# A decoder layer on one core: turnings by row count, parameter rows in one tile, sinks by a mask, two squares summed by accumulating transfers, state row copies apart

## The chip, the cores and the metric

The kernel runs on one core of a Trainium2 chip. A core has TensorE (PE: matrix products and turnings, that is transposes), VectorE (DVE), ScalarE (ACT), GpSimd (POOL) and SyncE (SP), each with its own in-order instruction stream, and DMA queues that move data between HBM and SBUF. The metric is the device time of one launch in microseconds, as the median of several runs; less is better.

## The reference

One inference step of a hybrid decoder layer, in float32, for 512 prompt tokens and 32 sample tokens (8 sequences of 4 tokens); D_MODEL is 1024, D_FF 4096:

```python
def _layer(x, ...):
    h = _rmsnorm(x, norm_mix_pre)
    x_r, q, k, v, g = split(h @ w_in)                    # one combined projection
    A = RG_LRU(causal_conv(x_r, width 4))                # 8 gate blocks
    B = window_attention(q, k, v)                        # window 128, 8 heads / 2 kv heads
    m = (sigmoid(g_A) * (A @ w_lru_o) + sigmoid(g_B) * (B @ w_attn_o)) @ w_out
    x = x + _rmsnorm(m, norm_mix_post)
    u = causal_conv(_rmsnorm(x, norm_ffn_pre) @ w_up, width 3)
    f = (gelu(u_gate) * u_val) @ w_down
    return x + _rmsnorm(f, norm_ffn_post)
```

In the attention each head has a sink, a number that joins the maximum and the denominator of the softmax, and a bias that depends on the distance in 32 buckets (`rel_bias`). The state rows (LRU state, convolution rows, the key and value window) are outputs too.

## The kernel before

**Numbers.** Each float32 operand of a product is split into a high and a low half (ScalarE makes the high one, VectorE the low one: `wh_*`/`wl_*` for weights, `hH`/`hL` for activations), and a product is three passes: high x high, high x low, low x high. Activations lie transposed: features on the 128 partitions, tokens along the free axis.

**Stages.** Up to 12 us: loads and the first turnings. Then the in-projection (`pmin`) with attention and LRU between its steps up to some 330 us; the two output products of the branches (`pmao`, `pmlo`); `w_out` (`pmout`, about 379 to 430 us); the norms behind it; and the feed-forward part, 430 to 965 us, where the up-projection runs in sums of weight blocks and of token halves (`pq` at first, later `pux`, `puy`, `puz`), the down-projection is `pmdn`, and the end turns the rows back and writes them.

**Order.** TensorE's stream is written out by hand for the whole program. In the first stages the other engines' streams are too: `step` (L344) emits one column block of a projection and then calls `tick` (L194), which runs the generators whose time has come (`start_at`, `sides`) and the lists `mids`, `late` and `last`. In the stage of `w_out` and the norms the tile scheduler orders ScalarE, VectorE and POOL, and `yield` in a generator sets how much TensorE work lies between its parts. Loads of weights go through SP's queue, each of them behind one of eight rotating semaphores; POOL issues its own transfers in its own stream, so that a transfer that waits holds up all that POOL does later.

**Places that the change touches.**
- `turn_b` (L521) turns tokens 256 to 543 to features: for each of four 128-column blocks k, two 128-row tiles and one 32-row tile (the sample tokens) into one PSUM bank `ps_tb`, two such groups of four k in all. The evictions (`hsplit`, `keep_b`) are put on `last` behind them. `xsquares` and `roots` (L533) work out the norm's factor; it is spread over the partitions by a product with a diagonal, `ps_rep <- dg, ones`.
- `relx` and `ohp` (L390 to L393) hold `rel_bias` and a one-hot matrix, 32 rows; their product in `roots` (bank `ps_rep`) picks the bias for each distance.
- `rows_a` and `rows_b` (L371, L573) hold norm and LRU parameters as rows; `params` (L596) turns them, the convolution weights `rows_f` and the state rows `st_rows` to columns.
- `sinkb` holds the sinks on all partitions, `sink8` as 8 rows; `sample_tables` (L659) makes `sinkr`, one sink for each row of the sample's score matrix, by a product with the mask `hsel`.
- `norm_chain` (L1234) works out the two norms behind `w_out` for one token half (a = 0 or 1, columns 0 to 271 and 272 to 543). For a = 1 it adds the scaled rows to the residual x (even c on POOL, odd c on VectorE), squares each of the eight x tiles on ScalarE (`sq_x`; the square of tile 0 goes straight to the sum `acc2`, called accx in the trace) and adds the squares on VectorE; `stats` sums over the partitions with a product (`pst_f`), `diag` and `spread` (`rep_f`) follow, and `normed` makes the operands of the next products. At the same time the splits of the first up-projection weights run on ScalarE and VectorE (`do_high`, `do_low`: `wh_e`, `wl_e`), for the products `pq` on TensorE.
- `ffn_states` (L1736) turns the last up-projected rows back near the end, copies them on ScalarE (`ffn_rows_s`, `ffn_rows_p`), and POOL writes them out.

The transfers that add what they carry to their target occur elsewhere too, in the sums of weight blocks (L1452 and L1453):

```python
pool.dma_start(out=w["p2"], in_=w["p1"], accum_op=ALU.add)
pool.dma_start(out=w["p4"], in_=w["p2"], accum_op=ALU.add)
```

Of the kernel before, what the change touches and what calls it, by code (L numbers as in the profile page):

```python
# [11 lines left out]
F32 = mybir.dt.float32  # L12
# [5 lines left out]
P = 128  # L18
# [11 lines left out]
NH = 8  # L30
# [60 lines left out]
def _shape_constants():  # L91
    t = np.arange(WIN)
    ohp = np.zeros((NBK, WIN), np.float32)
    ohp[_bucket(WIN - 1 - t), t] = 1.0
    ohs = np.zeros((DT, NBK, SKEY), np.float32)
    msk = np.full((2, DB // 2, NH, DT, SKEY), NEG, np.float32)
    for tq in range(DT):
        for kv in range(NKV):
            hs = slice(4 * kv, 4 * kv + 4)
            for j in range(WIN):  # L100
                dd = tq + WIN - j
                if 0 <= dd < WIN:
# [12 lines left out]
    return {  # L115
        "c_ohp": ohp,
        "c_ohs": ohs.reshape(DT * NBK, SKEY),
        "c_msk": msk.reshape(2, P, SKEY),
        "c_hsel": hsel.reshape(NH, P),
    }  # L120


# [1 line left out]
def hawk_step(ctx, tc, I, O):  # L124
# [21 lines left out]
    def T(name, dt=F32):  # L146
        return tp.tile([P, FLAT + 4], dt, tag="t", name=name)
# [7 lines left out]
    def PX(name):  # L155
        return psx.tile([P, 512], F32, tag="aux", name=name)
# [7 lines left out]
    def mm(out, l, r, start, stop):  # L164
        pe.matmul(out, l, r, start=start, stop=stop)  # L165
# [205 lines left out]
    rows_a = cp.tile([32, P], F32, name="rows_a")  # L371
    act.dma_start(out=rows_a[0:8, :], in_=I["norm_mix_pre"].rearrange("o (k p) -> (o k) p", p=P))
    warm = keep.tile([P, 1], F32, name="warm")
    act.activation(warm, epst, AF.Sqrt)
# [12 lines left out]
        nc.sync.dma_start(out=raw0[:, 4 * z:4 * z + 4, :], in_=wsrc(order[0])[:, 4 * z:4 * z + 4, :])  # L387
    wload(1)
    wload(2)
    relx = cp.tile([NBK, NH], F32, name="relx")  # L390
    nc.sync.dma_start(out=relx, in_=I["rel_bias"])
    ohp = T("ohp")[:NBK, 0:WIN]
    nc.sync.dma_start(out=ohp, in_=I["c_ohp"])  # L393
    wload(3)
    for i in (2, 3, 4):
        xload(i)
# [49 lines left out]
    def xtile(i, k):  # L446
        n = TOK[i][1]
        return xt[i, k // 4][:n, (k % 4) * P:(k % 4 + 1) * P]
# [70 lines left out]
    rq = cp.tile([P, 4], F32, name="rq")  # L519

    def turn_b(ks):  # L521
        for k in ks:
            ps = PX(f"ps_tb{k}")
            for i in (2, 3, 4):
                t0, n, _ = TOK[i]
                pe.transpose(ps[:, t0 - 256:t0 - 256 + n], xtile(i, k), ident[:n, :n])  # L526
            tb.append(ps)
            last.append(lambda k=k, ps=ps: hsplit(k, 1, ps[:, :288]))
        last.extend(lambda k=k, ps=tb[k]: keep_b(k, ps) for k in ks)

    ps_ohp = []
# [38 lines left out]
        yield from roots(2, 5)  # L570
        dve.tensor_scalar(rq, ss[:, 1, 0:4], SCALE, None, ALU.mult)

    rows_b = cp.tile([64, P], F32, name="rows_b")  # L573
    nc.sync.dma_start(out=rows_b[0:32, :], in_=I["conv_lru_w"].rearrange("o t (k p) -> (o t k) p", p=P))
    for r, nme in ((32, "conv_lru_b"), (40, "lru_br"), (48, "lru_bi"), (56, "lru_lambda")):
        nc.sync.dma_start(out=rows_b[r:r + 8, :], in_=I[nme].rearrange("o (k p) -> (o k) p", p=P))
# [18 lines left out]

    def params():  # L596
        ps = PX("ps_rows")
        pe.transpose(ps[:, 0:32], rows_a[:, :], ident[:32, :32])
        pe.transpose(ps[:, 32:96], rows_b[:, :], ident[:64, :64])
        pe.transpose(ps[:, 128:256], rows_f[:, 0, :], ident)  # L600
        pe.transpose(ps[:, 256:384], rows_f[:, 1, :], ident)
        px = PX("ps_st")
        for k in range(KD):
            pe.transpose(px[:, k * 32:(k + 1) * 32], st_rows[k // 4][:32, (k % 4) * P:(k % 4 + 1) * P], ident[:32, :32])
        yield
        dve.tensor_copy(pv[:, 8:96], ps[:, 8:96])
        dve.tensor_copy(fv, ps[:, 128:384])
# [27 lines left out]
    sink8 = cp.tile([NH, 1], F32, name="sink8")  # L635
    nc.sync.dma_start(out=sink8, in_=I["attn_sink"].rearrange("o h -> h o"))
    hsel = cp.tile([NH, P], F32, name="hsel")
# [21 lines left out]
    def sample_tables():  # L659
# [10 lines left out]
        yield 2  # L670
        ps = PX("ps_bs")
        mm(ps[:, 0:SKEY], lt.rearrange("p b h t -> p (b h t)"), ohs, True, True)
        mm(ps[:, 384:385], hsel, sink8, True, True)
        yield
        dve.tensor_copy(sinkr, ps[:, 384:385])
        for g in range(2):
            add(biasS[:, g, :], ps[:, 0:SKEY], mk[g])
        yield
# [555 lines left out]
    def norm_chain(a, acc):  # L1234
# [8 lines left out]
        with tc.high_priority(offset=HP):  # L1243
# [12 lines left out]
            for g in range(6 if a else 0):  # L1256
# [7 lines left out]
                for c in range(2 * g - 3, 2 * g - 1) if 1 <= g < 6 else ():  # L1264
                    if 0 <= c < 8:
                        sq[c] = acc2 if c == 0 else T(f"sq_x{a}_{c}")
                        act.activation(sq[c][:, :n], x1_(c), AF.Square)
                        if c == 0 and n % P:
                            pool.memset(acc2[:, n:n + P - n % P], 0.0)
                for c in range(2 * g - 5, 2 * g - 3) if g < 5 else range(5, 8):  # L1270
                    if c > 0:
                        add(acc2[:, :n], acc2[:, :n], sq[c][:, :n])
                yield 0.5
        yield NORM_TICKS[a]
# [461 lines left out]
    def ffn_states():  # L1736
        os_ = O["s_ffn_conv"].rearrange("o b i (m n) -> (o b i m) n", n=D)
        op = O["p_ffn_conv"].rearrange("o b i (m n) -> (o b i m) n", n=D)
        for kk in range(2):
# [4 lines left out]
                pe.transpose(py[:16, j * P:(j + 1) * P], stage_p[:, 4 * kk + j].rearrange("p r m -> p (r m)"), ident)  # L1744
            o1, o2 = S(f"ffn_rows_s{kk}"), S(f"ffn_rows_p{kk}")
            act.copy(o1[:, 0:512], px)
            act.copy(o2[:16, 0:512], py[:16, :])
            pool.dma_start(out=os_[:, kk * 512:(kk + 1) * 512], in_=o1[:, 0:512])
            pool.dma_start(out=op[:, kk * 512:(kk + 1) * 512], in_=o2[:16, 0:512])
# [230 lines left out]
```

## Time and profile before

| what | value |
|---|---|
| median of 3 runs | 993.14 us (993.14 to 993.22) |
| the profiled execution | 993.09 us |
| its span, first to last instruction | 991.3 us |
| mean granted TensorE clock | 0.999 |
| busy: ACT | 558.9 us (56%) |
| busy: POOL | 160.2 us (16%) |

All times in the trace are microseconds from the start of the span. A row of the timeline reads: start, duration, engine, line of the kernel, operation, output <- inputs, shape, number of instructions merged, and in brackets the idle time of the engine before it with what ended it. "PEld" is the loading of weights into TensorE, which runs beside the products. Products are pipelined, so that their listed durations overlap: the time that one costs is the step from its start to the next start. A wait ("idle") of another engine means nothing for the time unless TensorE, or the end, waits for what comes late.

### The profile page before, as it was taken

The numbers are of one execution on the slowest core, as the hardware profiler recorded it, in microseconds if no ns is written. First come the engines' busy times: TensorE is split into PE (matmuls) and PEld (weight loads), VectorE is DVE, ScalarE is ACT, GpSimd is POOL, SyncE is SP. The second block draws the span as 40 slices with busy tenths as digits, with TensorE's granted clock in tenths as the row PEclk, the third lists the DMA queues.
The fourth block names the chain that finished last, engine by engine and source line by source line (L and its number), as shares of the span: only waits on it lengthen the run. The fifth ranks groups of instructions, "written<-read, shape, count | busy, mean of one in ns | idle before, by whom it ended". The sixth has DMA issues, their size and how long they took to land.

```text
span 991.3 us, 20127 instructions
## 1 busy us (share of the span) xinstructions
PE 982.1 (99%) x7783; PEld 972.3 (98%) x7783; DVE 747.2 (75%) x1609; ACT 558.9 (56%) x1356; POOL 160.2 (16%) x269
## 2 busy tenths in 40 slices
PE   9999999999999999999999999999999999999997
PEld 8999999999999999999999999999999999999996
DVE  6777678766848655689786788887888888878766
ACT  6544433457466435556776655555655555556652
POOL 2152000001505341210001010101010101011004
PEclk9999999999999999999999999999999999999999
DMA  7675222323323534236048676767676767668612
GB/s 213 192 236 162 65 86 86 107 86 87 105 66 106 177 112 136 61 126 196 25 117 178 142 172 149 171 149 167 153 165 156 163 156 161 159 150 201 197 46 91
DMA packets 210999, 135.62 MB, mean 137 GB/s; under 512 B 8845, under 2 KB 197021, under 8 KB 210872
## 3 DMA queue, kind: packets, MB, share of 16 engines
q1 hardware_dynamic: 198920, 112.72, 40.0%
q0 software_dynamic: 11920, 19.59, 11.9%
q10 hardware_dynamic: 64, 2.04, 0.6%
q8 instruction: 61, 1.00, 0.4%
q14 instruction: 34, 0.28, 0.1%
HBM read 111.78 MB, written 11.37 MB: 124 GB/s over the span
## 4 chain that ended last, share of the span: by engine, by line
PE 96%; DVE 1%; ACT 1%; issue 0%; POOL 0%; DVEq 0%; ACTq 0%; POOLq 0%
PE pmin L165 22%; PE pmdn L165 17%; PE pux L1527 16%; PE puy L1527 8%; PE pq L1527 6%; PE pmout L165 5%; PE pmao L165 5%; PE pmlo L165 5%; PE puz L1527 4%; PE pg L165 1%; PE psc L165 1%; PE pvp L165 1%; PE ptok L165 1%; PE pt L820 1%; PE ps_warm L165 0%; PE ps_tb L526 0%
## 5 line engine op out<-in xcount | busy, mean ns | idle before, releaser
L165 PE MATMUL pmin<-hH,wh_in 128*128 128x256 f32 (+1 forms) x568 | 164.6, 292 | 0.0
L165 PE MATMUL pmin<-hL,wh_in 128*128 128x256 f32 (+1 forms) x568 | 162.3, 288 | 0.0
L165 PE MATMUL pmin<-hH,wl_in 128*128 128x256 f32 (+1 forms) x568 | 159.0, 288 | 0.0
L165 PE MATMUL pmdn<-fH,wh_dn 128*128 128x256 f32 (+1 forms) x448 | 129.3, 289 | 0.2 <-DVE ft L174 0.2
L165 PE MATMUL pmdn<-fH,wl_dn 128*128 128x256 f32 (+1 forms) x448 | 129.2, 288 | 0.0
L165 PE MATMUL pmdn<-fL,wh_dn 128*128 128x256 f32 (+1 forms) x448 | 128.8, 287 | 0.0
L177 DVE SCALAR_TENSOR_TENSOR uc<-u,fv,uc 128x560 f32<-128x560 f32 x128 | 102.0, 797 | 13.3 <-ACT uc L1558 13.2
L165 PEld LDWEIGHTS pmin<-hH,wh_in 128*128 128x128 f32 x568 | 107.2, 189 | 1.4 <-issue 1.2
L165 PEld LDWEIGHTS pmin<-hL,wh_in 128*128 128x128 f32 x568 | 107.3, 189 | 0.1
L165 PEld LDWEIGHTS pmin<-hH,wl_in 128*128 128x128 f32 x568 | 104.7, 188 | 0.2 <-issue 0.2
L165 PEld LDWEIGHTS pmdn<-fH,wh_dn 128*128 128x128 f32 x448 | 84.3, 188 | 0.6 <-issue 0.6
L165 PEld LDWEIGHTS pmdn<-fL,wh_dn 128*128 128x128 f32 x448 | 84.4, 188 | 0.0
L165 PEld LDWEIGHTS pmdn<-fH,wl_dn 128*128 128x128 f32 x448 | 84.4, 188 | 0.0
L1655 ACT COPY u<-pux 128x272 f32<-128x272 f32 x52 | 20.1, 386 | 84.1 <-PE pux L1527 84.1
L168 DVE TENSOR_TENSOR u<-puy,u 128x240 f32<-128x240 f32 (+2 forms) x78 | 24.6, 344 | 49.4 <-PE puy L1527 32.5
L283 ACT ACTIVATE wh_in<-raw_in 128x512 fp32r<-128x512 f32 x70 | 42.8, 627 | 31.7 <-issue 18.1
L174 DVE TENSOR_TENSOR ft<-ft,pmdn 128x256 f32<-128x256 f32 (+1 forms) x104 | 45.2, 435 | 17.3 <-PE pmdn L165 16.8
L290 DVE TENSOR_TENSOR wl_in<-raw_in,wh_in 128x512 fp32r<-128x512 f32 x70 | 48.0, 697 | 1.0 <-ACT wh_in L283 1.0
L1558 ACT ACTIVATE uc<-u,fv 128x560 f32<-128x560 f32 x64 | 48.3, 756 | 0.0
L1453 POOL DMA_DIRECT2D raw_up_s<-raw_up_s x26 | 22.7, 872 | 101.1 <-DMA raw_up_s<-raw_up__10513 4.5
L168 DVE TENSOR_TENSOR wl_dn<-raw_dn,wh_dn 128x512 fp32r<-128x512 f32 x56 | 38.3, 684 | 0.0
L165 PE MATMUL pmout<-mH,wh_out 128*128 128x272 f32 x128 | 37.5, 293 | 0.0
(779 smaller groups left out, 3380.3 us busy)
## 6 DMA issues: line engine op xcount, KB each, us to landing
raw_in<-in_w_in_dram SPq DMA_DIRECT2D x35, 512.0 KB
raw_dn<-in_w_down_dram SPq DMA_DIRECT2D x56, 256.0 KB
raw_up_s<-in_w_up_dram SPq DMA_DIRECT2D x25, 512.0 KB
raw_up_s<-raw_up_s POOLq DMA_DIRECT2D x26, 256.0 KB, 5.7
raw_ao<-in_w_attn_o_dram SPq DMA_DIRECT2D x8, 512.0 KB
raw_lo<-in_w_lru_o_dram SPq DMA_DIRECT2D x8, 512.0 KB
raw_out<-in_w_out_dram SPq DMA_DIRECT2D x8, 512.0 KB
xdram<-xn POOLq DMA_DIRECT2D x8, 272.0 KB, 8.3
```

The costliest lines, as they stand in the source:

```text
L165: pe.matmul(out, l, r, start=start, stop=stop)
L168: dve.tensor_tensor(out=out, in0=a, in1=b, op=ALU.subtract)
L174: dve.tensor_tensor(out=out, in0=a, in1=b, op=ALU.add)
L177: dve.scalar_tensor_tensor(out=out, in0=a, scalar=s_, in1=b, op0=op0, op1=op1)
L283: act.activation(hl[0], raw, AF.Copy)
L290: (eng or dve).tensor_tensor(out=hl[1], in0=raw, in1=f32(hl[0]), op=ALU.subtract)
L820: pe.transpose(pt[:, (2 * ch + j) * P:(2 * ch + j + 1) * P], s3[:, j, ch * P:(ch + 1) * P], ident)
L1453: pool.dma_start(out=w["p4"], in_=w["p2"], accum_op=ALU.add)
L1527: pe.matmul(ps[:, :HN], w, x, start=start and k == 0 and i == 0, stop=stop and k == 3 and i == 2, skip_group_check=True)
L1558: act.activation(yt[j][:, 0:FLATU], u[:, 0:FLATU], AF.Copy, scale=fv[:, j:j + 1])
L1655: act.copy(e[nm_], z)
```

## The change

Six edits:
1. `turn_b` takes its four banks first, then turns the 128-row tiles of all four k, then the four 32-row tiles. The evictions follow in the order they had.
2. `relx` and `ohp` get 128 rows, set to zero by POOL before the loads of the first 32 rows.
3. `rows_b` becomes rows 32 to 95 of `rows_a`: one turning of 96 rows in place of one of 32 and one of 64. The 128-row turnings of `rows_f` move behind those of `st_rows`.
4. The product of `hsel` and `sink8` goes, and the load of `sink8`. `hsel` is loaded as 128 x 8, and one VectorE instruction multiplies it by `sinkb` and sums along the row into `sinkr`, where a copy from PSUM stood.
5. For a = 1 the squares of tiles 2 and 3 are added to that of tile 1 by two transfers that POOL issues, from SBUF to SBUF (128 x 272 values, 136 KB each). VectorE adds tiles 4, 5, 6, the sum from 1, and 7 to `acc2`: five adds where seven were, later in its stream.
6. In `ffn_states` a `yield 0.5` stands between the two copies.

```diff
-    relx = cp.tile([NBK, NH], F32, name="relx")
-    nc.sync.dma_start(out=relx, in_=I["rel_bias"])
-    ohp = T("ohp")[:NBK, 0:WIN]
-    nc.sync.dma_start(out=ohp, in_=I["c_ohp"])
+    relx = cp.tile([P, NH], F32, name="relx")
+    pool.memset(relx, 0.0)
+    nc.sync.dma_start(out=relx[:NBK, :], in_=I["rel_bias"])
+    ohp = T("ohp")[:, 0:WIN]
+    pool.memset(ohp, 0.0)
+    nc.sync.dma_start(out=ohp[:NBK, :], in_=I["c_ohp"])
...
     def turn_b(ks):
+        tb.extend(PX(f"ps_tb{k}") for k in ks)
+        for group in ((2, 3), (4,)):
+            for k in ks:
+                for i in group:
+                    t0, n, _ = TOK[i]
+                    pe.transpose(tb[k][:, t0 - 256:t0 - 256 + n], xtile(i, k), ident[:n, :n])
         for k in ks:
-            ps = PX(f"ps_tb{k}")
-            for i in (2, 3, 4):
-                t0, n, _ = TOK[i]
-                pe.transpose(ps[:, t0 - 256:t0 - 256 + n], xtile(i, k), ident[:n, :n])
-            tb.append(ps)
-            last.append(lambda k=k, ps=ps: hsplit(k, 1, ps[:, :288]))
+            last.append(lambda k=k, ps=tb[k]: hsplit(k, 1, ps[:, :288]))
...
-    rows_b = cp.tile([64, P], F32, name="rows_b")
+    rows_b = rows_a[32:96, :]
...
     def params():
         ps = PX("ps_rows")
-        pe.transpose(ps[:, 0:32], rows_a[:, :], ident[:32, :32])
-        pe.transpose(ps[:, 32:96], rows_b[:, :], ident[:64, :64])
-        pe.transpose(ps[:, 128:256], rows_f[:, 0, :], ident)
-        pe.transpose(ps[:, 256:384], rows_f[:, 1, :], ident)
+        pe.transpose(ps[:, 0:96], rows_a[:, :], ident[:96, :96])
         px = PX("ps_st")
         for k in range(KD):
             pe.transpose(px[:, k * 32:(k + 1) * 32], st_rows[k // 4][:32, (k % 4) * P:(k % 4 + 1) * P], ident[:32, :32])
+        for z in range(2):
+            pe.transpose(ps[:, (z + 1) * P:(z + 2) * P], rows_f[:, z, :], ident)
...
         mm(ps[:, 0:SKEY], lt.rearrange("p b h t -> p (b h t)"), ohs, True, True)
-        mm(ps[:, 384:385], hsel, sink8, True, True)
-        yield
-        dve.tensor_copy(sinkr, ps[:, 384:385])
+        yield
+        dve.scalar_tensor_tensor(out=hsel, in0=sinkb, scalar=1.0, in1=hsel, op0=ALU.mult, op1=ALU.mult, accum_out=sinkr)
...
                         act.activation(sq[c][:, :n], x1_(c), AF.Square)
                         if c == 0 and n % P:
                             pool.memset(acc2[:, n:n + P - n % P], 0.0)
-                for c in range(2 * g - 5, 2 * g - 3) if g < 5 else range(5, 8):
-                    if c > 0:
+                        if c in (2, 3):
+                            pool.dma_start(out=sq[1][:, :n], in_=sq[c][:, :n], accum_op=ALU.add)
+                for c in ((), (), (), (), (4,), (5, 6, 1, 7))[g]:
+                    if c:
                         add(acc2[:, :n], acc2[:, :n], sq[c][:, :n])
...
             act.copy(o1[:, 0:512], px)
+            yield 0.5
             act.copy(o2[:16, 0:512], py[:16, :])
```

How the built program's order moves is shown at two places. The first is TensorE's stream at the first group of `turn_b`, behind the last product of an in-projection step (`pmin`); x are the token tiles as they were loaded, `ps_tb` the banks. Before:

```order
L165 MATMUL pmin_0_420<-hH_165,wl_in_401 128x256
L526 MATMUL ps_tb_453<-ident,x_0_122 128x128
L526 MATMUL ps_tb_453<-ident,x_0_126 128x128
L526 MATMUL ps_tb_453<-ident,x_0_130 128x32
L526 MATMUL ps_tb_457<-ident,x_0_122 128x128
L526 MATMUL ps_tb_457<-ident,x_0_126 128x128
L526 MATMUL ps_tb_457<-ident,x_0_130 128x32
```

After:

```order
L529 MATMUL ps_tb_454<-ident,x_0_128 128x128
L529 MATMUL ps_tb_455<-ident,x_0_124 128x128
L529 MATMUL ps_tb_455<-ident,x_0_128 128x128
L529 MATMUL ps_tb_452<-ident,x_0_132 128x32
L529 MATMUL ps_tb_453<-ident,x_0_132 128x32
L529 MATMUL ps_tb_454<-ident,x_0_132 128x32
L529 MATMUL ps_tb_455<-ident,x_0_132 128x32
L165 MATMUL pmin_0_490<-hH_153,wh_in_446 128x256
```

The twelve turnings are the same; the 32-row ones (shape 128x32, from the sample tile) now stand together at the end, and the first bank is whole only with the ninth turning.

The second place is the norm of a = 1. On POOL, before:

```order
L1261 TENSOR_TENSOR x_0_4624<-x_0_4624,mt_5226 128x272
L1261 TENSOR_TENSOR x_2_4626<-x_2_4626,mt_5228 128x272
L1261 TENSOR_TENSOR x_4_4628<-x_4_4628,mt_5230 128x272
L1261 TENSOR_TENSOR x_6_4630<-x_6_4630,mt_5232 128x272
L1452 DMA raw_up_s<-raw_up__6390 128x512
```

After:

```order
L1260 TENSOR_TENSOR x_0_4621<-x_0_4621,mt_5223 128x272
L1260 TENSOR_TENSOR x_2_4623<-x_2_4623,mt_5225 128x272
L1270 DMA sq_x_1_6016<-sq_x_2_6018 128x272
L1260 TENSOR_TENSOR x_4_4625<-x_4_4625,mt_5227 128x272
L1270 DMA sq_x_1_6016<-sq_x_3_6044 128x272
L1260 TENSOR_TENSOR x_6_4627<-x_6_4627,mt_5229 128x272
```

The second transfer, which waits for the first one's landing since both add into the same tile, stands ahead of the add of tile 6. On VectorE the same stage (`wl_e` are the low halves of the up-projection weights, accx the sum) reads before:

```order
L174 TENSOR_TENSOR x_7_4631<-x_7_4631,mt_5233 128x272
L174 TENSOR_TENSOR accx_5966<-accx_5966,sq_x_1_6019 128x272
L174 TENSOR_TENSOR accx_5966<-accx_5966,sq_x_2_6021 128x272
L168 TENSOR_TENSOR wl_e_0_6053<-raw_up__5714,wh_e_0_6052 128x512
L174 TENSOR_TENSOR accx_5966<-accx_5966,sq_x_3_6046 128x272
L174 TENSOR_TENSOR accx_5966<-accx_5966,sq_x_4_6048 128x272
L168 TENSOR_TENSOR wl_e_1_6077<-raw_up__5712,wh_e_1_6076 128x512
L174 TENSOR_TENSOR accx_5966<-accx_5966,sq_x_5_6068 128x272
L174 TENSOR_TENSOR accx_5966<-accx_5966,sq_x_6_6070 128x272
L174 TENSOR_TENSOR accx_5966<-accx_5966,sq_x_7_6094 128x272
```

After:

```order
L174 TENSOR_TENSOR x_7_4628<-x_7_4628,mt_5230 128x272
L168 TENSOR_TENSOR wl_e_0_6050<-raw_up__5711,wh_e_0_6049 128x512
L174 TENSOR_TENSOR accx_5963<-accx_5963,sq_x_4_6047 128x272
L168 TENSOR_TENSOR wl_e_1_6073<-raw_up__5709,wh_e_1_6072 128x512
L174 TENSOR_TENSOR accx_5963<-accx_5963,sq_x_5_6065 128x272
L174 TENSOR_TENSOR accx_5963<-accx_5963,sq_x_6_6067 128x272
L174 TENSOR_TENSOR accx_5963<-accx_5963,sq_x_1_6016 128x272
L174 TENSOR_TENSOR accx_5963<-accx_5963,sq_x_7_6090 128x272
```

The adds of squares 1, 2 and 3 have left the front, so that `wl_e_0` follows the last x at once; the add of square 1, which now carries the sum of three, stands last but one and waits for the second transfer.

More of the change, by code (lines that the diff above doesn't have):

```diff
@@ L118, in _shape_constants @@
         "c_msk": msk.reshape(2, P, SKEY),
-        "c_hsel": hsel.reshape(NH, P),
+        "c_hsel": np.ascontiguousarray(hsel.reshape(NH, P).T),
     }
@@ L369, in hawk_step @@
     TOK = [(i * P, P, xp[i * P:(i + 1) * P, :]) for i in range(4)] + [(SEQ, NS, xs)]
-    rows_a = cp.tile([32, P], F32, name="rows_a")
+    rows_a = cp.tile([96, P], F32, name="rows_a")
     act.dma_start(out=rows_a[0:8, :], in_=I["norm_mix_pre"].rearrange("o (k p) -> (o k) p", p=P))
@@ L634, in hawk_step @@
     nc.sync.dma_start(out=sinkb, in_=I["attn_sink"].partition_broadcast(P))
-    sink8 = cp.tile([NH, 1], F32, name="sink8")
-    nc.sync.dma_start(out=sink8, in_=I["attn_sink"].rearrange("o h -> h o"))
-    hsel = cp.tile([NH, P], F32, name="hsel")
+    hsel = cp.tile([P, NH], F32, name="hsel")
     nc.sync.dma_start(out=hsel, in_=I["c_hsel"])
```

## The prediction

> **What bounds the kernel now.** I read the page first: the busy line, then the chain that ended last.
>
> ```profile
> PE 982.1 (99%) x7783; PEld 972.3 (98%) x7783; DVE 747.2 (75%) x1609; ACT 558.9 (56%) x1356; POOL 160.2 (16%) x269
> PE 96%; DVE 1%; ACT 1%; issue 0%; POOL 0%; DVEq 0%; ACTq 0%; POOLq 0%
> ```
>
> TensorE is busy for 99% of the span and 96% of the chain is its own. Whatever shortens the stream of TensorE instructions is worth its full length, and whatever lets TensorE wait costs its full length; work of other engines counts only where TensorE waits for it. So the next view is the list of TensorE's waits. Beside the two waits in the first microseconds it has three rows:
>
> ```profile
> PE pq L1527 <- DVE wl_e L168: 0.4, 1, 0.4
> PE pmdn L165 <- ACT ffn_rows_s L1746: 0.4, 1, 0.4
> PE pmdn L165 <- DVE ft L174: 0.2, 1, 0.2
> ```
>
> They add up to 1.0 us, so removed waits can hardly pay much. What remains are small losses inside the TensorE stream that are not listed as waits. The timeline of the weight loads (start, duration, instruction, how many merged, idle time before) shows them at the turnings of `turn_b`:
>
> ```profile
> 21.80 0.38 PEld L526 LDWEIGHTS ps_tb<-ident,x 32*128 32x128 f32 x3 [0.17 <-issue]
> 22.35 0.38 PEld L526 LDWEIGHTS ps_tb<-ident,x 32*128 32x128 f32 x3 [0.17 <-issue]
> ```
>
> Each 32-row turning stands behind 0.17 us in which the weight loader waits for nothing visible, and the pattern of two 128-row turnings and one 32-row one repeats every 22.35 - 21.80 = 0.55 us. Without a change of row count, turnings go faster:
>
> ```profile
> 949.12 0.60 PE L1730 MATMUL px<-ident,x1r 128*128 128x128 f32 x4
> 949.56 0.27 PE L1743 MATMUL pfs<-ident,sfT 128*128 128x128 f32 x1
> ```
>
> Four of 128 rows take 949.56 - 949.12 = 0.44 us, 0.11 each. For those of 32 rows the parameter turnings serve:
>
> ```profile
> 42.56 0.29 PE L165 MATMUL pmin<-hH,wl_in 128*128 128x288 f32 x1
> 42.78 0.25 PE L598 MATMUL ps_rows<-ident,rows_a 32*128 32x32 f32 x1
> 43.53 0.68 PE L604 MATMUL ps_st<-ident,st_rows 32*128 32x32 f32 x8
> 44.13 0.33 PE L724 MATMUL pk<-ident,klast 128*128 128x128 f32 x1
> ```
>
> Eight of 32 rows and the step back to 128 rows take 44.13 - 43.53 = 0.60 us. With some 0.17 for the step back (the idle time above), (0.60 - 0.17)/7 = 0.06 each is left.
>
> **The change, part by part.**
>
> *Turnings by row count.* In `turn_b` one tile column costs 0.55 now and would cost 2 x 0.11 + 0.06 = 0.28 without the two steps, so a round trip between the row counts costs 0.27. Four per group become one: 3 x 0.27 = 0.8 saved, in two groups 1.6.
>
> [...]
>
> *Parameters.* From the last `pmin` to `pk` now 44.13 - 42.56 = 1.57 us, with four changes of row count (to 32, 64, 128, 32 rows and back to 128: 0.22 from 42.56 to 42.78 alone, where a `pmin` step is 0.13). Afterwards one 96-row turning, eight 32-row ones, two 128-row ones follow in this order: 0.13 + 0.20 (step to 32 rows) + 7 x 0.06 + 0.17 (step back) + 0.16 + 0.11 = 1.2. Saved: 0.4. That 96 rows run as 128 do is not in the trace; if they are a mode of their own, 0.2 is left.
>
> *The bucket product.* `ohp` and `relx` grow from 32 rows to 128:
>
> ```profile
> 17.18 0.38 PE L165 MATMUL ps_rep<-ohp,relx 32*8 32x128 f32 x2
> 18.57 0.37 PE L165 MATMUL pmin<-hH,wh_in 128*128 128x256 f32 x1
> ```
> ```profile
> 17.60 0.37 ACT L550 COPY rep<-ps_rep 128x256 f32<-128x256 f32 x1 [3.14 <-PE ps_rep L165]
> 17.86 1.16 ACT L283 ACTIVATE wh_in<-raw_in 128x512 fp32r<-128x512 f32 x2
> ```
>
> One round trip, 0.27, goes; but the `pmin` at 18.57 needs the `wh_in` that ScalarE makes after its copy of `ps_rep`, and that copy moves only by the step in, about 0.1. I take 0.2, between 0.1 and 0.27. The two memsets run on POOL before the loads that would wait for them have reached the head of SP's queue (these also wait for the first input rows), so they cost nothing; with that cover gone it would be their own fractions of a microsecond.
>
> *Sinks.* The 8-row product goes:
>
> ```profile
> 62.38 0.70 PE L165 MATMUL ps_bs<-ohs,lt 128*128 128x320 f32 x2
> 63.01 0.38 PE L165 MATMUL ps_bs<-sink,hsel 8*128 8x1 f32 x2
> 63.32 0.38 PE L165 MATMUL psc<-kH,qH 128*128 128x256 f32 x1
> ```
>
> The product holds TensorE from 63.01 to 63.32, and a step into 8 rows (some 0.1) and a slow restart lie around it: 0.47, between 0.31 and 0.6. On VectorE an 8-column operation replaces a copy of one column; it no longer waits for TensorE. I take nothing for it. One small load leaves SP's queue: what follows it comes earlier, and TensorE waits for no load there.
>
> Together TensorE's stream shrinks by 1.6 + 0.4 + 0.2 + 0.47 = 2.65 us before 64 us. Not all of it arrives. Between the two parts of `turn_b` and the rest stands the root of tokens 256 to 543:
>
> ```profile
> 35.16 0.65 PE L165 MATMUL ps_rep<-dg,ones 128*128 128x288 f32 x2
> ```
> ```profile
> 33.39 0.71 DVE L540 TENSOR_SCALAR dg<-ident,ss 128x128 f32<-128x128 f32 x3
> ```
>
> `dg` is done at 34.10, 1.06 before TensorE needs it. TensorE will come 1.6 + 0.2 = 1.8 earlier, while the chain to `dg` (evictions of the turned banks, squares, root) starts when the first bank is whole, which is now only after eight large turnings and a small one: it comes some 0.3 earlier. So TensorE now waits 1.8 - 1.06 - 0.3 = 0.44. After that nothing holds it up to 430 us (no row in the waits). Net of the first part: 2.65 - 0.45 = 2.2, between 1.7 and 2.7.
>
> *The squares.* This is the only part that can lose. In the second norm (tokens of columns 272 to 543) VectorE runs the sum and the low halves `wl_e` side by side:
>
> ```profile
> 443.41 0.72 DVE L174 TENSOR_TENSOR x<-x,mt 128x272 f32<-128x272 f32 x1
> 444.05 0.90 DVE L174 TENSOR_TENSOR accx<-accx,sq_x 128x272 f32<-128x272 f32 x2
> 444.88 0.68 DVE L168 TENSOR_TENSOR wl_e<-raw_up__5714,wh_e 128x512 fp32r<-128x512 f32 x1
> 446.91 1.46 DVE L174 TENSOR_TENSOR accx<-accx,sq_x 128x272 f32<-128x272 f32 x3
> ```
> ```profile
> 445.62 0.39 PE L1527 MATMUL pq<-b11H,wl_e 128*128 128x272 f32 x1 [0.40 <-DVE wl_e L168]
> 448.48 0.77 PE L165 MATMUL pst_f<-ones,accx 128*128 128x1 f32 x6
> ```
>
> The `wl_e` of 444.88 is the one TensorE waits for at 445.62, and the sum is complete at 446.91 + 1.46 = 448.37, only 0.1 before `pst_f`. Two adds of 0.45 leave VectorE, and `wl_e` comes first now, so up to 0.66 could be won here (the 0.40 of waiting and the slow restart). Against it stand two transfers on POOL's in-order queue. Their inputs are ready early, and behind the second one waits POOL's add `x_6`:
>
> ```profile
> 439.53 0.43 ACT L1267 ACTIVATE sq_x<-x 128x272 f32<-128x272 f32 x1 [0.61 <-POOL x L1261]
> 443.86 0.43 ACT L1267 ACTIVATE sq_x<-x 128x272 f32<-128x272 f32 x1 [0.90 <-POOL x L1261]
> 444.20 0.62 ACT L1464 ACTIVATE wh_e<-raw_up__5712 128x512 fp32r<-128x512 f32 x1
> ```
> ```profile
> 443.05 0.79 POOL L1261 TENSOR_TENSOR x<-x,mt 128x272 f32<-128x272 f32 x1 [1.39 <-DVE mt L177]
> ```
>
> The first transfer issues when the third square ends, 439.53 + 0.43 = 439.96, say 440.0. With L1 and L2 for the times from the issue to the landing, the second issues at 440.0 + L1 (it waits for the first, as both add into one tile), `x_6` comes 0.87 behind that issue (below), and ScalarE's `sq_6`, `wh_e` and what follows move with `x_6`. The sum ends at 440.0 + L1 + L2 and two more adds of 0.45, and `pst_f` follows 0.1 later. It stands at 448.48 now, so it shifts by 440.0 + L1 + L2 + 1.0 - 448.48 = L1 + L2 - 7.5, but never below what VectorE and TensorE need themselves.
>
> The trace has no transfer of 136 KB between SBUF tiles with an add. The nearest rows are the accumulating ones of 256 KB and a plain one of 12 KB (`rscr`):
>
> ```profile
> 520.73 0.86 POOL L1452 DMA_DIRECT2D raw_up_s<-raw_up__7031  x1 [13.02 <-ACT wh_s_a L1464]
> 525.82 0.88 POOL L1453 DMA_DIRECT2D raw_up_s<-raw_up_s  x1 [4.23 <-DMA raw_up_s<-raw_up__7031]
> 18.92 0.74 POOL L656 DMA_DIRECT2D rscr<-rvec  x1 [7.17 <-DVE rvec L655]
> 21.25 1.13 POOL L682 DMA_DIRECT2D rrep<-rscr  x1 [1.60 <-DMA rscr<-rvec]
> raw_up_s<-raw_up_s POOLq DMA_DIRECT2D x26, 256.0 KB, 5.7
> ```
>
> 12 KB took 21.25 - 18.92 = 2.3 us from issue to landing, 256 KB took 525.82 - 520.73 = 5.1 there and 5.7 in the median of the dependent ones. In between, by bytes: 2.3 + 124/244 x 2.8 = 3.7 us for 136 KB. The windows give the load of the transfer engines in both places:
>
> ```profile
> 441.00:444.00 3.00, 3.00 (x26) 3.00 (x25) 2.93 (x6) 1.41 (x4) 1.44 (x2) 1.00 1.06 369
> 520.70:525.80 5.10, 5.10 (x43) 5.10 (x42) 2.59 (x8) 2.22 (x5) 0.86 (x1) 1.00 0.93 184
> ```
>
> The next to last column is the share: 1.06 against 0.93, since the `x1d` rows are written just then. So I take 3.7 for the first and 4.2 for the second: a shift of 3.7 + 4.2 - 7.5 = +0.4. The ends are 2.3 twice (the shift by the sum is -2.9, so it decides nothing, and the 0.66 is won) and 5.7 twice (+3.9).
>
> *State rows.* The wait of 0.4 at `pmdn` is named after the ScalarE copy `ffn_rows_s`. But the `ft` add ends next to it:
>
> ```profile
> 946.85 0.45 DVE L174 TENSOR_TENSOR ft<-ft,pmdn 128x288 f32<-128x288 f32 x1
> ```
>
> It ends at 947.30, and TensorE's next row starts behind a 0.37 us idle that ends just after that; the add frees the bank. A `yield` between two copies therefore moves ScalarE work that TensorE does not wait for: 0, at most 0.2 either way.
>
> **Sum.** 993.09 (the profiled execution; its span is 991.3, with 1.8 around it) - 2.2 + 0.4 + 0 = 991.3 us. The median of the runs shown is 993.14, so 0.05 above.
>
> **Rivals.** *B, the transfers are hidden.* If a landing takes 3.4 or less, the sum is no longer late and VectorE's relief counts: -2.2 - 0.66 = -2.9, and 990.2 us; 989.8 if the wait for `dg` doesn't come either. For it: the transfers are half as large as the accumulating ones, and 12 KB needed only 2.3. Against it: the load of 1.06.
>
> [...]
>
> *C, the transfers are slow.* One mechanism: they queue behind the `x1d` writes, POOL stands at the second, `x_6`, `sq_6` and `wh_e` come late, and TensorE stops at `pst_f`. At 5.7 each the shift is +3.9 and the time 993.09 - 2.2 + 3.9 = 994.8; at 6.7 each +5.9 and 996.8. It cancels the gain from L1 + L2 = 9.7 on and is slower by over 0.2% from 11.7 on. For it: the dependent transfers of 256 KB had 5.7 in the median. Against it: half the bytes.
>
> *D, the turnings give less.* If the round trips are shorter than the rows make them look, because a chain outside TensorE (evictions, `dg`, `wh_in`) holds the next product anyway, only parameters and sinks remain, 0.9: 993.09 - 0.9 + 0.4 = 992.6. Against it: no TensorE wait stands in the rows there.
>
> **How the numbers follow.** Forecast 0.48 (its own range 990.4 to 992.2), B 0.28, C 0.10, D 0.14. 0.2% is 1.99 us, about what a measurement of this kernel can tell from no change: below 991.15 is faster. Of the forecast half (0.24) lies there, and all of B: 0.52. The other half and D make 0.38 for the same, C 0.10 for slower. The range goes from B's lower end, 989.8, to 993.2 above D.
>
> **What would show it.** In the changed profile: the weight loads of each `turn_b` group with one idle of 0.17 in place of four, and the first `pmin` after the first group 0.8 earlier; a wait at `ps_rep<-dg` of about 0.4; `psc` straight behind `ps_bs<-ohs,lt`; at 430 us everything 2.2 earlier; two POOL transfers with 3.7 and 4.2 us between issue and landing, and a TensorE wait at `pst_f` or just before it. It is wrong if TensorE's lead at 430 us is below 1.5 or above 3, if `pst_f` loses over 1.5 us, or if work behind `pst_f` (the operands of the next products) waits as well.

## The result and the profile after

| | before | changed |
|---|---|---|
| median | 993.14 us (993.04 to 993.22, 6 runs) | 997.40 us (994.67 to 998.20, 6 runs) |
| profiled execution, its span | 993.09, 991.3 us | 998.10, 996.3 us |
| granted clock, mean | 0.999 | 0.993 |

The change makes the kernel slower: the ratio is 1.0038, with an interval of 1.0024 to 1.0051. The forecast was 991.3, and its range ended at 993.2. Two things besides the time are new. The runs of before lie within 0.2 us, those of the changed kernel within 3.5. And the mean granted clock is lower.

The page of the changed kernel, busy line and clock line (40 slices of 24.9 us, in tenths of full speed):

```profile
PE 985.0 (99%) x7780; PEld 976.5 (98%) x7780; DVE 745.5 (75%) x1608; ACT 557.8 (56%) x1356; POOL 162.1 (16%) x273
...
PEclk9999999999999999998999999999999999999999
```

TensorE has fewer instructions than before and still 2.9 us more busy time. One slice, the 19th (448 to 473 us), has a clock digit below 9: its products took longer. TensorE's waits, against the list before and beside the two of the first microseconds, have one new row, and the 0.4 at `pq <- DVE wl_e` is gone:

```profile
PE pq L1528 <- ACT wh_e L1465: 2.8, 1, 2.8
PE ps_warm L165 <- POOL ones L219: 1.0, 1, 1.0
PE pm_first L165 <- DVE wh_in L285: 0.6, 1, 0.6
PE pmdn L165 <- ACT ffn_rows_s L1747: 0.4, 1, 0.4
PE pmdn L165 <- DVE ft L174: 0.2, 1, 0.2
```

To see where time comes and goes, I subtracted the start of each TensorE instruction before from that of the same one after (minus: earlier than before):

| instruction | before | after | shift |
|---|---|---|---|
| second product of `psc`, behind the sinks | 63.54 | 61.47 | -2.07 |
| `pq`, the one that waited 0.40 for `wl_e` | 445.62 | 442.98 | -2.64 |
| first `pq <- b21H, wh_e` behind it | 446.99 | 447.18 | +0.19 |
| `rep_f` | 452.21 | 457.06 | +4.85 |
| last turning of the end | 984.87 | 989.74 | +4.87 |

The lead of 2.1 us is won by 64 us and stays to the norm, where 0.6 more is won. Then 2.8 us are lost in one wait and 4.7 in the 10 us behind it. Nothing happens after 457 us. The changed kernel's POOL timeline shows how it starts:

```profile
438.18 0.94 POOL L1270 DMA_DIRECT2D sq_x<-sq_x  x1 [0.77 <-ACT sq_x L1266]
438.85 1.08 POOL L1260 TENSOR_TENSOR x<-x,mt 128x272 f32<-128x272 f32 x1
444.47 0.89 POOL L1270 DMA_DIRECT2D sq_x<-sq_x  x1 [4.54 <-issue]
445.11 1.04 POOL L1260 TENSOR_TENSOR x<-x,mt 128x272 f32<-128x272 f32 x1
```

The second transfer issues at 444.47, 6.3 us behind the first (whose last part, by the semaphore's events, landed at 443.92), and the add of `x_6` stands behind it. POOL's "issue" idle of 4.54 is that landing. ScalarE and TensorE follow:

```profile
440.82 0.41 ACT L1266 ACTIVATE sq_x<-x 128x272 f32<-128x272 f32 x1
446.18 0.43 ACT L1266 ACTIVATE sq_x<-x 128x272 f32<-128x272 f32 x1 [4.94 <-POOL x L1260]
446.51 0.61 ACT L1465 ACTIVATE wh_e<-raw_up__5709 128x512 fp32r<-128x512 f32 x1
```
```profile
444.12 0.28 PE L1528 MATMUL pq<-b11H,wl_e 128*128 128x272 f32 x1
447.18 0.59 PE L1528 MATMUL pq<-b21H,wh_e 128*128 128x272 f32 x1 [2.78 <-ACT wh_e L1465]
...
448.53 0.43 PE L1528 MATMUL pq<-b21L,wh_e 128*128 128x272 f32 x1
448.75 0.43 PE L1528 MATMUL pq<-b21H,wl_e 128*128 128x272 f32 x1
```

`sq_6` starts at 446.18, `wh_e` stands behind it in ScalarE's stream, and TensorE needs that `wh_e` at 444.24 (the row at 444.12 and one step of 0.12). The two last rows show the other loss: the step is 0.22 us, where it was 0.125 before. The windows give the granted clock (the third number from the end; the last two are the share of the transfer engines and GB/s):

```profile
443.00:444.20 1.20, 1.20 (x12) 1.19 (x10) 0.09 (x1) 0.00 (x0) 0.00 (x0) 1.00 0.55 206
447.20:450.00 2.80, 2.80 (x11) 2.57 (x12) 2.63 (x6) 2.37 (x6) 0.00 (x0) 0.50 1.01 325
453.00:456.00 3.00, 3.00 (x15) 3.00 (x15) 1.51 (x5) 0.62 (x2) 0.00 (x0) 0.50 0.61 175
457.00:460.00 3.00, 3.00 (x24) 2.92 (x23) 2.21 (x5) 1.11 (x2) 0.00 (x0) 0.99 0.56 141
```

It is 0.50 from 446.81 to 457.06, by the clock's own events in the trace.

### The profile page after: what moved, and what is told of

The parts are those of the page before. It is cut to its first block, busy times and chain, and to the rows that moved or that the text cites. A ratio compares the mean times of both kernels' runs of the same rounds, so it can differ in the third digit from the quotient of the medians.

```text
span 996.3 us, 20129 instructions
## 1 busy us (share of the span) xinstructions
PE 985.0 (99%) x7780; PEld 976.5 (98%) x7780; DVE 745.5 (75%) x1608; ACT 557.8 (56%) x1356; POOL 162.1 (16%) x273
## 4 chain that ended last, share of the span: by engine, by line
PE 96%; ACT 1%; DVE 1%; issue 1%; POOL 0%; DMA 0%; DVEq 0%; ACTq 0%; POOLq 0%
PE pmin L165 22%; PE pmdn L165 17%; PE pux L1528 16%; PE puy L1528 8%; PE pq L1528 7%; PE pmout L165 5%; PE pmao L165 5%; PE pmlo L165 5%; PE puz L1528 4%; PE pg L165 1%; PE psc L165 1%; PE pvp L165 1%; PE ptok L165 1%; PE pt L819 1%; PE ps_warm L165 0%
## 5 line engine op out<-in xcount | busy, mean ns | idle before, releaser
L776 ACT ACTIVATE s<-s,st 128x256 f32<-128x256 f32 (+1 forms) x32 | 15.2, 475 | 40.7 <-DVE st L773 23.1
```

The costliest lines, as they stand in the source:

```text
L776: act.activation(s3[:, j, :], s3[:, j, :], AF.Exp, bias=ng[:, j:j + 1], accum_out=sm[:, j:j + 1])
```

## The experiments

Theory: five of the six edits gain about 2 us; the transfers hold POOL, `x_6`, `sq_6` and `wh_e` in turn; TensorE waits; and the wait is followed by a half clock. Each experiment below takes one link of that away or makes one alone. "Before" beside them had a median of 993.2 us on each occasion.

| label | what it is | median, range (us) | ratio to before, interval |
|---|---|---|---|
| e1_sums_undone | change without the transfers | 991.10, 991.02 to 991.88 | 0.9981, 0.9972 to 0.9990 |
| e2_only_transfers | before with the transfers alone | 998.81, 996.69 to 999.08 | 1.0051, 1.0039 to 1.0064 |
| e3_fill | change, TensorE kept busy | 994.89, 993.60 to 995.95 | 1.0016, 1.0007 to 1.0025 |
| e4_pool_adds | POOL adds in place of transfers | 991.10, 990.74 to 991.88 | 0.9979, 0.9970 to 0.9988 |
| e5_delay8 | before, `x_6` late by POOL work | 1000.49, 999.76 to 1000.55 | 1.0072, 1.0057 to 1.0087 |
| e6_delay13 | the same, later still | 1002.67, 1002.41 to 1003.56 | 1.0097, 1.0082 to 1.0112 |
| e7_x1d_late | change, `x1d` writes held back | 998.84, 998.32 to 1001.30 | 1.0062, 1.0047 to 1.0077 |
| e8_x6_on_dve | change, `x_6` on VectorE | 999.75, 998.93 to 999.93 | 1.0064, 1.0047 to 1.0080 |
| e9_pool_adds_apart | POOL adds, each in a gap of POOL | 990.48, 990.24 to 991.32 | 0.9973, 0.9962 to 0.9983 |
| e10_turn_b_only | before with `turn_b` alone | 992.10, 991.70 to 992.96 | 0.9989, 0.9980 to 0.9998 |
| e11_delay6 | as e5, shorter | 995.93, 995.64 to 996.97 | 1.0029, 1.0018 to 1.0040 |
| e12_one_transfer | change with one transfer | 991.22, 990.99 to 992.12 | 0.9980, 0.9971 to 0.9989 |

### The transfers taken away, and alone

e1 puts the old loop back into the changed kernel, e2 puts the new one into the kernel before:

```diff
-                        if c in (2, 3):
-                            pool.dma_start(out=sq[1][:, :n], in_=sq[c][:, :n], accum_op=ALU.add)
-                for c in ((), (), (), (), (4,), (5, 6, 1, 7))[g]:
-                    if c:
+                for c in range(2 * g - 5, 2 * g - 3) if g < 5 else range(5, 8):
+                    if c > 0:
```

> The changed kernel with the second norm's squares summed as before (seven VectorE adds, no transfers). Theory: all the loss sits in the two transfers, and the other five edits keep the lead of 2.06 us that the trace of the change shows at 64 us (shift of psc). Then the profiled execution lies near 991.1 us, without a TensorE wait at pq and with a granted clock of 0.999. Rival: the other edits also lose something later (the order at the end, 950 us); then it is above 992.

> The kernel before with the two accumulating transfers alone. Theory (transfer under load holds POOL, then TensorE waits 2.8 us, then a half clock for some 10 us): the loss of the change after 445 us, 2.8 + 4.5 less the 0.6 that VectorE's relief wins, shows here too, 997 to 1000 us with a TensorE wait of 2 to 3.5 us at pq, and runs that differ by several us. Rival (the loss needs the earlier arrival of TensorE by 2 us): the wait is below 1.5 us and the time below 995.

Measured: 991.10 and 998.81, both as the theory had it. In e1 the 0.4 us wait at `pq <- DVE wl_e` is back, which I had not expected, and none is added; the last turning of its profiled execution starts 1.88 us earlier than that of before. In e2 the wait is

```profile
PE pq L1529 <- ACT wh_e L1466: 2.6, 1, 2.6
```

and the clock is at one half from 449.46 to 456.29. So the transfers carry the whole loss, +5.6 us in e2 against before and +6.3 from e1 to the changed kernel, and the other five edits are a gain of 2.1.

### Is the half clock a consequence of the wait?

e3 fills TensorE's wait with 11 products of a tile of zeros, which add nothing; e5, e6 and e11 make waits of several lengths in the kernel before, with no transfer in the norm (eight multiplications in e5, shown; thirteen in e6, six in e11):

```diff
...
+                if (z, u, j) == (4, 1, early[4]):
+                    for _ in range(FILLS):
+                        pe.matmul(qps[j, 0][:, :P], zero, ones, start=False, stop=False, skip_group_check=True)
                 plain("e", j, u, 0)
```
```diff
                         pool.tensor_tensor(out=x1_(c), in0=x1_(c), in1=m_, op=ALU.add)
+                    for _ in range(8 if c == 6 else 0):
+                        pool.tensor_tensor(out=x1_(c)[:, :P], in0=x1_(c)[:, :P], in1=ones, op=ALU.mult)
```

> The changed kernel with 11 products of a zero tile by a tile of ones on TensorE, added into the open bank just ahead of the pq that waits; what is computed stays the same. They occupy TensorE for roughly 2.7 us while it would wait. Theory (the half clock follows from the idle stretch): the products behind the wait step at 0.125 us again, the 4.5 us go, and the time is 993 to 994 us with runs close together. Rival (the half clock comes from the load of the transfers or from the time itself): the steps stay at 0.227 us and the time near 997.4.

> The kernel before, without any transfer in the norm, but with eight POOL multiplications of half of x_6 by ones behind its add, about 0.42 us each and 3.4 us together. x_6 reaches ScalarE 3.4 us late, the wh_e behind it ends at 448.2 instead of 444.8, and TensorE, which needs it at 446.99, waits 1.2 us. Theory (a wait of 2.8 us halves the clock, a short one doesn't): no half clock, 994.4 to 995.2 us, runs close together. Rival 1 (any wait at this place is followed by the half clock): 998 or more. Rival 2 (lateness of x_6 isn't the path; the sum's landing is): the time stays near 993.1.

> As before, with thirteen such multiplications, 5.5 us: TensorE waits about 3.3 us at the same place, without any transfer. Theory: the half clock follows for some 10 us and costs about 4.5 us, in most runs: 998 to 1001.5 us, runs that differ by some us, PEclk 0.50 in the windows behind the wait. Rival (the half clock comes from the transfers, not from the idle): 993.1 + 3.5 = 996.6 us and PEclk 1.00.

> The kernel before with six multiplications of half of x_6 by ones on POOL, 0.62 us each as the run with eight showed, 3.7 us together: TensorE waits about 0.9 us in the place where it waited 2.1 us with eight, and up to 1.1 us at the wl_e before it. Theory (the clock is lowered when a stretch of 3.4 us on a fixed grid holds too much idle): about 2 us of idle spread over two stretches leave the clock at 1.00, 994.5 to 995.5 us. Rival (this much is enough): PEclk 0.50 again, 998 to 1000 us.

TensorE's timeline in e3: the fillers, what follows, and a window behind them.

```profile
444.11 2.62 PE L1765 MATMUL pq<-ones,zero 128*128 128x128 f32 x22
446.92 0.39 PE L1531 MATMUL pq<-b21H,wh_e 128*128 128x272 f32 x1 [0.19 <-ACT wh_e L1468]
447.14 0.28 PE L1531 MATMUL pq<-b21L,wh_e 128*128 128x272 f32 x1
447.64 0.39 PE L1531 MATMUL pq<-b21H,wl_e 128*128 128x272 f32 x1 [0.21 <-DVE wl_e L169]
447.87 0.29 PE L1531 MATMUL pq<-b21H,wh_e 128*128 128x272 f32 x1
447.99 0.29 PE L1531 MATMUL pq<-b21L,wh_e 128*128 128x272 f32 x1
```
```profile
450.00:452.00 2.00, 2.00 (x17) 2.00 (x18) 1.90 (x9) 1.62 (x5) 0.00 (x0) 1.00 0.98 290
```

The transfers are those of the changed kernel, their load is much the same (0.98 in this window, 1.08 there), and the wanted product starts only 0.26 us earlier (446.92 for 447.18), but the clock stays at 1.00 and the step at 0.125. The median falls by 2.5 us to 994.89, less far than the 993 to 994 that I had expected, the profiled execution from 998.10 to 994.31. What is left, 3.8 us above e1, is the wait and the late sum.

e5, TensorE's two waits and a window behind them:

```profile
446.39 0.39 PE L1529 MATMUL pq<-b11H,wl_e 128*128 128x272 f32 x1 [1.07 <-DVE wl_e L168]
449.98 0.59 PE L1529 MATMUL pq<-b21H,wh_e 128*128 128x272 f32 x1 [2.06 <-ACT wh_e L1466]
```
```profile
450.00:452.00 2.00, 2.00 (x7) 1.77 (x8) 1.86 (x5) 2.00 (x6) 0.00 (x0) 0.50 0.32 115
```

e11, the same with six multiplications:

```profile
446.38 0.39 PE L1529 MATMUL pq<-b11H,wl_e 128*128 128x272 f32 x1 [1.06 <-DVE wl_e L168]
448.90 0.40 PE L1529 MATMUL pq<-b21H,wh_e 128*128 128x272 f32 x1 [1.00 <-ACT wh_e L1466]
449.63 0.39 PE L1529 MATMUL pq<-b21H,wl_e 128*128 128x272 f32 x1 [0.20 <-DVE wl_e L168]
```
```profile
450.00:452.00 2.00, 2.00 (x18) 1.93 (x17) 1.90 (x4) 1.43 (x4) 0.00 (x0) 1.00 0.76 264
```

A multiplication took 0.62 us instead of the 0.42 that I had set, so e5's waits were longer than meant: 2.06 in place of 1.2, and 1.07 at the `wl_e` before it, which VectorE made late beside POOL's work (the two adds ahead of it took 1.32 us instead of 0.90, and it took 0.93 itself instead of 0.68). It had the half clock, which I had expected only in e6. That is rival 1's number; but e11 has a wait at the same place and no half clock, so the step lies between these two. One us less of waiting (1.00 for 2.06) saved 4.6 us of time, since the half clock went with it. The 995.93 is still 0.4 above the range of the theory, and one of the six runs (996.97) lists a mean clock of 0.996: a half clock in that one, which was not traced, isn't excluded. e6 waited 4.7 us, had the half clock too, and came out above its 1001.5 for the same reason as e5. No transfer is needed: rival 2 of e5 (only the landing of the sum matters) and the rival of e6 (the half clock comes from the transfers) fall.

### What makes the first transfer slow, and what stands behind it

```diff
+            nc.sync.dma_start(out=x1d[:, 0, 0:1], in_=dg[0:8, 0:1])
             for c in range(8):
                 nc.sync.dma_start(out=x1d[c], in_=x1[c][:, 0:NT])
```
```diff
-                    if c % 2 == 0:
+                    if c == 6:
+                        add(x1_(c), x1_(c), m_)
+                    elif c % 2 == 0:
```

> The changed kernel with a transfer of eight numbers from the diagonal dg_f into x1d ahead of the eight x1d writes, so that these start only after about 453 us; what they write stays the same. Theory (the first accumulating transfer is slow because the x1d writes fill the engines): it lands in 2.7 to 3.5 us instead of 5.7, x_6 is about 1 us late, TensorE waits less than 0.7 us, no half clock, 990.5 to 992 us. Rival (an accumulating transfer takes 5.7 us by itself the first time): landing and time as in the changed kernel, 995 to 998. Later loads on the same queue may come late and add to either.

> The changed kernel with the add of x_6 on VectorE, so that nothing of the norm stands behind the second transfer on POOL. Theory (the loss is x_6, sq_6 and wh_e behind the transfer): the wait at pq goes, but the sum still lands late: the second transfer lands at about 447.2, two adds follow, and TensorE waits about 2.4 us at pst_f, which it reaches at 445.85. Without a half clock 992.9 us; with it up to 997.4: this wait is the shorter one, so it also shows how long an idle stretch may be. Rival (the landing doesn't matter): 990.5 to 991.

POOL in e7, then in e8:

```profile
438.08 0.94 POOL L1270 DMA_DIRECT2D sq_x<-sq_x  x1 [0.77 <-ACT sq_x L1266]
438.74 1.08 POOL L1260 TENSOR_TENSOR x<-x,mt 128x272 f32<-128x272 f32 x1
445.23 0.88 POOL L1270 DMA_DIRECT2D sq_x<-sq_x  x1 [5.40 <-issue]
```
```profile
439.06 0.94 POOL L1272 DMA_DIRECT2D sq_x<-sq_x  x1 [0.77 <-ACT sq_x L1268]
439.73 1.08 POOL L1262 TENSOR_TENSOR x<-x,mt 128x272 f32<-128x272 f32 x1
446.41 0.89 POOL L1272 DMA_DIRECT2D sq_x<-sq_x  x1 [5.60 <-ACT wh_e L1467]
```

e7 missed both ranges: 998.84 us. The `x1d` writes are gone from this stretch, and the second issue still comes 7.1 us behind the first: other loads of the same queue moved up (a 512 KB block of `w_up`, issued at 436.07, and the 512 KB of state rows at 438.23). So it isn't these writes alone, and I haven't separated which traffic slows it. What the six runs with such transfers do show is that the time goes with the load. Where the engines' share was about 0.4 or less (the second transfer in the changed kernel, e2, e3 and e7), 136 KB landed 2.7 us after the issue, with the first data 1.45 us after it. At shares of 0.7 to 1.03 (the first in all six, the second in e8) it took 5.0 to 6.8 us, with the first data 2.5 to 3.3 us after the issue. Within this second group the share doesn't order the times: 0.68 came with 6.6 us in e7, 1.03 with 5.6 in e12 and with 6.8 in e8.

In e8 nothing waits at `pq` any more, but the sum itself is later than I had worked out: the second transfer, which again issues 0.55 us behind the landing of the first (445.86, whatever releaser the row names), lands 5.0 us after its issue, not 2.7. Beside it (share 0.82) run most of the 512 KB of state rows and the next 512 KB block of `w_up`, which SP issued at 444.36 and 445.07. In the changed kernel they issued at 447.07 and 447.88, behind `x1d` writes that stood waiting for the late `x_6`.

```profile
PE pst_f L165 <- DVE accx L174: 5.4, 1, 5.4
```

Half clock again (450.90 to 457.73), 999.75 us, above both of my values. So `x_6` behind the transfer is only one of two ways to lose; the sum is the other, and the late `x_6` happened to hold back the traffic that slowed the second transfer here.

### Relief for VectorE without two landings in a row

e4 and e9 let POOL add where the transfers stood, e12 keeps one transfer (e9 shown; in e4 both adds go into `sq[1]`, from 2 and 3; in e12 only c == 2 is transferred and VectorE adds 3 and 4, then 5, 6, 1, 7):

```diff
-                        if c in (2, 3):
-                            pool.dma_start(out=sq[1][:, :n], in_=sq[c][:, :n], accum_op=ALU.add)
-                for c in ((), (), (), (), (4,), (5, 6, 1, 7))[g]:
+                        if c in (2, 4):
+                            pool.tensor_tensor(out=sq[c - 1][:, :n], in0=sq[c - 1][:, :n], in1=sq[c][:, :n], op=ALU.add)
+                for c in ((), (), (), (), (1,), (3, 5, 6, 7))[g]:
```

> The changed kernel with two POOL adds (about 0.8 us each) in place of the two transfers. Theory: POOL has 1.4 us idle between its adds, so x_6 is not late, VectorE keeps its relief, and wl_e comes early enough that the wait of 0.4 at pq goes: 993.14 - 2.06 - 0.55, about 990.5 us. Rival (POOL's adds slow VectorE's, or x_4 and x_6 come late by the adds' 1.6 us): 991 to 992.

> The changed kernel with two POOL adds in place of the transfers, one (square 2 into 1) between the adds of x_2 and x_4, the other (square 4 into 3) between x_4 and x_6; VectorE adds 1, 3, 5, 6, 7. Theory: POOL is idle for 1.4 us in each of these places, so neither x_4 nor x_6 is late, as x_4 was when both adds stood ahead of it; wl_e comes before TensorE needs it and the wait of 0.4 at pq goes: 0.55 below the run with the sums undone, about 990.5 us. Rival (VectorE runs slower beside POOL's adds, so the relief is given back): 991.0 to 991.2.

> The changed kernel with one transfer instead of two: square 2 is added to square 1 by the transfer, square 3 by VectorE, which then has six adds. Nothing on POOL waits for a landing. Theory (the loss is POOL's next issue standing ahead of x_6, not the transfer): the transfer still lands 5 to 6 us after its issue, at about 444, which is ahead of the sum's use by VectorE at about 446, there is no wait at pq and no half clock, 990.6 to 991.1 us. Rival (a transfer of this kind in the loaded stretch costs TensorE time in itself): a wait at pq or pst_f and over 993 us.

POOL in e9:

```profile
437.41 0.78 POOL L1260 TENSOR_TENSOR x<-x,mt 128x272 f32<-128x272 f32 x1 [1.39 <-DVE mt L177]
438.73 1.00 POOL L1270 TENSOR_TENSOR sq_x<-sq_x,sq_x 128x272 f32<-128x272 f32 x1 [0.54 <-ACT sq_x L1266]
439.69 0.77 POOL L1260 TENSOR_TENSOR x<-x,mt 128x272 f32<-128x272 f32 x1
441.00 0.99 POOL L1270 TENSOR_TENSOR sq_x<-sq_x,sq_x 128x272 f32<-128x272 f32 x1 [0.54 <-ACT sq_x L1266]
441.96 0.77 POOL L1260 TENSOR_TENSOR x<-x,mt 128x272 f32<-128x272 f32 x1
```

In e4 the scheduler put both adds ahead of `x_4`, which came 1.0 us late; `wl_e` was no earlier, the wait of 0.4 stayed, and the time is that of e1: the rival held. In e9 each add fits between two x, the shift against before moves from -1.31 to -1.87 at that `pq`, and the time is 990.48, below both kernels and below e1 by 0.6. (The intervals of e9 and e1 overlap; the trace shows where the gain arises.) (The profiled execution of e9, 991.32, is one of its slower ones, with a wait of 0.4 at `pmin <- DVE ks` early on.)

e12 shows the same transfer in the same load without harm. Its issue row, and TensorE at `pst_f`:

```profile
sq_x<-sq_x POOLq DMA_DIRECT2D x1, 136.0 KB, 5.6
```
```profile
446.20 0.83 PE L165 MATMUL pst_f<-ones,accx 128*128 128x1 f32 x6 [0.25 <-DVE accx L174]
```

It takes 5.6 us, and nothing waits for it: 991.22, 0.1 above the theory's range and far from the rival's. The gain of 0.5 at `wl_e` is given back at `pst_f`, as six VectorE adds end later than five. The loss in the change is therefore the second issue, which waits for the first landing.

### The first part by itself

> The kernel before with the turnings of turn_b by row count alone. In the trace of the change the two groups gain 1.4 to 1.5 us and about 0.3 is lost again at the products with dg and wh_in by 40 us. Theory (the groups' own steps pay, nothing else depends on them): a lead of 1.1 to 1.2 at 64 us, 992.0 us. Rival (TensorE merely waits later, since the chain to dg doesn't come earlier): 992.8 to 993.1.

e10 carries the new `turn_b` into the kernel before. Measured 992.10, with a lead of 1.45 behind the second group that shrinks to 1.13 by 40 us and stays: the theory's number.

## Why the prediction was wrong

**What held.** The first part, term by term, from the shifts: the two groups of `turn_b` 1.5 (forecast 1.6); loss behind them 0.3, in two places, at `ps_rep` and near 39.5 us (forecast 0.44 at `ps_rep`); parameters 0.44 (0.4; the 96-row turning starts 0.13 us behind the 128-row product ahead of it, 41.55 after 41.42, and the weight loader has no idle before it, where it has 0.17 before the 32-row ones); sinks 0.49 (0.47). The bucket product gave nothing that the shifts show (0.2 forecast): the shift stays at +0.07 from 7.6 to 22 us. The sum, 2.07 by the trace and 2.1 by e1, was forecast as 2.2, and nothing of it was lost up to 430 us. VectorE's relief won 0.6 at the `wl_e` wait, as rival B had it. The state rows changed nothing at the end. (Two slips of the prediction move nothing: its four parts add to 2.67, not 2.65, and the parameters' stretch has five changes of row count, not four.)

**What failed is the step on the squares**, in three places.

1. *The landing.* I took 3.7 us for the first transfer from a line between 12 KB and 256 KB. It took 5.74, rival C's price, and POOL's next issue came 6.29 behind the first. The second, which I put at 4.2 because of the `x1d` writes, took 2.71: little ran beside it (76 GB/s in all, share 0.39, from 444.2 to 447.2 us), as SP's `x1d` writes stood waiting for the late `x_6`. The two errors cancel in large part in the sum L1 + L2, and that was the only place where I gave them a price.

2. *The path.* I wrote that `sq_6` and `wh_e` move with `x_6`, and then priced only the end of the sum, L1 + L2 - 7.5. With the measured values that gives 6.29 + 2.71 - 7.5 = +1.5 us. The true path runs from L1 alone through `x_6`, `sq_6` and `wh_e`, and TensorE needs that `wh_e` twelve products, 1.5 us, ahead of `pst_f`. In e3, where no half clock blurs it, `pst_f` came 3.2 us late (from a lead of 2.2 to a lag of 1.0). Rival C named this chain, but priced it in the same wrong place and needed both transfers to be slow.

3. *The clock.* I priced a wait at its length, and what follows it at nothing. The wait of 2.8 us was followed by 10.2 us at half speed. Between the profiled executions of the changed kernel and e3 that is 3.8 us; between the medians it is 2.5. The changed kernel's spread of 3.5 us is in keeping with it: the six runs have clocks from 0.993 (998.1) to 0.998 (994.67), in step with their times.

## What to carry to other kernels

A transfer on POOL's queue that must wait for another one's landing is a wait for everything that POOL does later (the add of `x_6` started 6.9 us behind the first issue here, 445.11 for 438.18); before adding one, list what stands behind it in that stream, and follow each of these to TensorE separately, not only the value that is transferred. Price landings by the load of the transfer engines at that moment, from a row with the same load (136 KB took 2.7 us at a share of about 0.4, 5.0 to 6.8 at 0.7 to 1.03), and keep two dependent ones out of a busy stretch. And on a kernel that keeps TensorE busy for 99% of the time, a wait of some 2 us can cost more than its length, since the clock may drop behind it: e5 lost 7.3 us to 3.1 us of waiting, while e11, which kept the clock, lost 2.7 to 2.3. Where such a wait can't be avoided, products that add zero can keep the clock up, as in e3 (1.00 from 450 to 452 us, where the changed kernel had 0.50).

## What the runs showed of the hardware

By the clock's events in its trace, the changed kernel ran 440.32 us at full clock, 10.24 at half and 535.89 at full; the kernel before ran 983.04 us at full clock. These are 129, 3, 157 and 288 times 3.413 us. The stretch at half clock was 10.24 us in e5 and e6 too, and 6.83 in e2, e7 and e8, two times 3.41. Each began 1.0 (e5, with another wait shortly before) to 4.9 us (e7) after TensorE had run dry, in e2 and e7 when it had already gone on.

Waits of 2.06 us (e5, 1.5 us behind another one of 1.07), 2.6 (e2), 2.8 (the changed kernel), 3.65 (e7), 4.7 (e6) and 5.4 (e8) were followed by the half clock. A wait of 1.00 us (e11, 1.5 us behind another one of 1.06) was not, nor were the three of 0.19 to 0.33 in e3 and the 0.40 in the kernel before. No run lies between e11 and e5. That the idle time is counted over a stretch of 3.4 us on a fixed grid, as the theory of e11 has it, was my assumption: e11 agrees with it, and would have come out the same if only the longest wait counted.

The full clock came back 5.2 us (e8: from 452.56 to 457.73) to 9.9 us (the changed kernel: from 447.18 to 457.06) after TensorE had gone on. The same kernel differs from run to run: the mean clocks of the changed kernel's six runs go from 0.993 to 0.998.

A change of row count on TensorE and back cost (0.07 + 1.45) / 6 = 0.25 us, an estimate from the shifts and the six round trips that left the two groups. The weight loader's idle of 0.17 us before the 32-row turnings, four in the first group before, stands there once in the changed kernel.
